# A further pair of weight columns by seven products, and pairs whose second result goes through SBUF, in a one-core hybrid decoder trunk

## The chip, the cores and the metric

The kernel runs on one core of one Trainium2 chip. The metric is the time of one execution on the device, in microseconds (us); the median of several executions is given. A core has five engines that work side by side, each through its own queue in order: TensorE (PE in the profile, with the loading of its weights as PEld), VectorE (DVE), ScalarE (ACT), GpSimd (POOL) and SyncE (SP), which here issues most DMA transfers. SBUF is the on-chip memory, PSUM the memory into which TensorE writes.

## The reference

One layer of a decoder trunk over 256 tokens of width 2048, in float32. A combined input projection feeds two token mixers (a gated delta rule over 16 heads of 128, and a causal pooling mixer); their results are merged through gates, projected out and added; then follows a gated MLP of width 5632 with a causal depthwise convolution.

```python
h = rmsnorm(x, norm_mix_w[l])
proj = jnp.einsum('bsd,de->bse', h, w_in[l])
q, k, v, z, b_raw, a_raw, p_in, g_a, g_b = jnp.split(proj, splits, axis=-1)
qkv = jax.nn.silu(causal_dwconv(jnp.concatenate([q, k, v], axis=-1), conv_qkv_w[l]))
...
o = gated_delta_rule(q, k, v, g_log, beta)
o = rmsnorm(o, gdn_norm_w[l]) * jax.nn.silu(z)          # per head
pooled = causal_multiscale_pool(p_in)                   # 4 groups of 512 channels
y_b = jnp.einsum('bsgc,gcd->bsgd', pooled, pool_w[l]) * pool_scale[l]
mixed = jax.nn.sigmoid(g_a) * y_a + jax.nn.sigmoid(g_b) * y_b
x = x + jnp.einsum('bsd,de->bse', mixed, w_out[l])
h = rmsnorm(x, norm_ffn_w[l])
...                                                     # gated MLP, final norm
```

## The kernel before

**Stages.** The input projection is worked off in four groups of 512 channels (four heads, one pooling window). Each group passes K, Q, V, P (the pooling mixer's input), GB (its gate), Z, the pooling product, and GA (the delta rule's gate), each a product of 256 tokens by 2048 by 512. Then come the output projection, the MLP's up and down projections and the last norm. The delta rule of a group is side work: a generator (`gdn`, line 948 and after) that advances by one step whenever a product calls `side()`; `LATE[g]` is the number of steps that it lets pass before it starts the triangular solve.

**A weight tile.** Weights come in tiles of 128 x 1024 (two blocks of 128 rows by 512 columns). Each is loaded by SP into `raw` (four buffers), rounded by ACT to a high half (`whi`, line 357, a cast) and split by DVE into a low half (`wlo`, line 368, raw minus high). `weights()` does this a few tiles ahead of the product that uses them, in the order of the list `srcs`. A plain tile costs PE twelve matmuls of 128x512 (two blocks, two token halves, and high by high, low by high, high by low: lines 416 to 418 in `gemm_a`).

**A pair by seven products.** Where two columns of weights are multiplied by the same tokens, a stretch of 512 rows of both (four tiles of 128 x 1024: 11, 12, 21, 22, here called the quad) is done by seven products of six matmuls in place of four plain tiles of twelve, a Strassen-like scheme: the operands T1 to T4 are sums of quarters, formed in place by DVE (`up_sum`, line 284), and the tokens' sums are made once. The seven are called T1, 11, T2, 21, T3, 22 and T4; each has its own cast and split. `pair_product` (line 423 and after) issues one of them on line 455 and moves partial results: after T1 ACT copies bank a's half to SBUF (`own`), after 11 ACT copies the other half over, after T2 DVE adds `own` to the half and keeps the sum in SBUF (`u`, line 443), after T3 DVE adds `own` again and writes it into the second bank of PSUM (line 445). At 21 ACT copies u into the second bank. T3 writes the PSUM half that u is read from, so T3 waits for the addition of u.

Such pairs exist before for K and Q of groups 1 to 3, with T1, 11 and T2 set among the last tiles of the GA before (`KQ_FIRST`), 21, T3 and 22 one behind the other (`KQ_MIDDLE`), and the rest among the plain tiles that follow (`KQ_THEN`), and likewise for two columns of the output projection; others stand in the MLP, which the change leaves alone.

**The running sums.** In group 0 the gate's running sums (16 x 256) are written to DRAM (`crd`, line 817), read back spread over the partitions (`crow`, line 969), masked by POOL (line 974), and become decays by eight exponentials on ACT (`dec`, line 982). A convolution's taps on DVE are `cy` (line 934).

**What sets the order.** Most instructions are put in order on each engine by the scheduler of the language from the order of the code and its own costs; `issue_after` adds an edge, and `manual_schedule` keeps the written order.

## Time and profile before

| what | before |
|---|---|
| median of 3 runs | 1524.24 us (1523.72 to 1524.89) |
| profiled execution | 1524.25 us |
| its span, first to last instruction | 1522.5 us |
| granted TensorE clock | 0.999 |
| busy: PE, PEld, DVE, ACT, POOL | 1513.1, 1250.8, 1287.0, 896.1, 75.0 us |
| starts of tiles in group 0: V's last, P's first | 81.68, 84.42 us |

The profiled execution is the median one, within 0.01 us; 1.75 us of it lie around the span. Matmuls overlap, so their durations add up to more than their pace, and the pace is read from their starts. A row of a timeline gives the start, the duration, engine, line and operation, output and inputs; several alike in a row are put together (x2), and behind them in brackets stands the idle time of the engine before the row and what ended it.

### The profile page before, as it was taken

What the parts mean: (1) busy time and instruction counts of PE and PEld (TensorE: products, weight loads), DVE (VectorE), ACT (ScalarE), POOL (GpSimd) and SP (SyncE); (2) the same over time, 40 slices, a digit from 0 to 9 for tenths busy, and PEclk for the clock granted to TensorE, in tenths of its full rate; (3) what the DMA queues carried; (4) which work ended last, traced back from release to release, by engine and by line L of the source; (5) the groups of instructions that cost most, each with busy time, mean ns of one, the idle gap of its engine ahead of it and who ended that gap; (6) DMA issues with size and microseconds to landing.
All of it is one profiled execution on the core that took longest, in us unless ns stands there. A gap on an engine that the chain in (4) does not pass through costs nothing.

```text
span 1522.5 us, 20282 instructions
## 1 busy us (share of the span) xinstructions
PE 1513.1 (99%) x7260; PEld 1250.8 (82%) x7260; DVE 1287.0 (85%) x1799; ACT 896.1 (59%) x1160; POOL 75.0 (5%) x97
## 2 busy tenths in 40 slices
PE   9999999999999999999999999999999999999998
PEld 8888888888878888888888888888888888888886
DVE  6779868888688878888777999999998886989896
ACT  7456556455646456456465676667666665555562
POOL 1000001000100001000000000000000011010100
PEclk9999999999999999999999999999999999999999
DMA  8777647784677747774678656666457468566662
GB/s 277 209 226 221 207 139 225 235 255 115 198 221 218 227 127 219 214 238 154 217 227 303 198 164 218 221 212 216 152 164 238 142 212 276 172 223 219 220 220 100
DMA packets 170099, 313.62 MB, mean 206 GB/s; under 512 B 23650, under 2 KB 27010, under 8 KB 169870
## 3 DMA queue, kind: packets, MB, share of 16 engines
q1 hardware_dynamic: 160864, 283.17, 59.0%
q0 software_dynamic: 7344, 27.27, 5.5%
q10 hardware_dynamic: 1790, 1.89, 0.4%
q8 instruction: 57, 0.93, 0.2%
q14 instruction: 44, 0.36, 0.1%
HBM read 303.33 MB, written 8.95 MB: 205 GB/s over the span
## 4 chain that ended last, share of the span: by engine, by line
PE 98%; DVE 1%; issue 1%; ACT 0%; POOL 0%; POOLq 0%; DVEq 0%
PE psg L455 28%; PE psm L418 14%; PE psm L416 14%; PE psm L417 14%; PE psm L1644 8%; PE psg L1644 7%; PE psm L455 4%; PE psm L606 1%; PE psm L1712 1%; PE psg L505 1%; PE psg L993 1%; DVE wlo L368 1%; PE psg L995 0%; PE psm L521 0%; PE psg L1139 0%
## 5 line engine op out<-in xcount | busy, mean ns | idle before, releaser
L357 ACT CAST whi<-raw 128x1024 fp32r<-128x1024 f32 x400 | 419.9, 1052 | 311.0 <-PE psm L417 157.9
L368 DVE TENSOR_TENSOR wlo<-raw,whi 128x1024 fp32r<-128x1024 f32 x398 | 484.1, 1220 | 119.3 <-ACT whi L357 113.9
L357 ACT CAST whi<-quad 128x1024 fp32r<-128x1024 f32 x217 | 227.9, 1053 | 167.5 <-PE psg L455 46.2
L368 DVE TENSOR_TENSOR wlo<-quad,whi 128x1024 fp32r<-128x1024 f32 x217 | 263.4, 1220 | 39.9 <-ACT whi L357 34.8
L416 PE MATMUL psm<-whi,xhl 128*128 128x512 f32 x384 | 150.0, 391 | 0.0
L417 PE MATMUL psm<-whi,xhl 128*128 128x512 f32 x384 | 149.9, 390 | 0.0
L418 PE MATMUL psm<-wlo,xhl 128*128 128x512 f32 x384 | 139.0, 393 | 0.0
L455 PE MATMUL psg<-whi,fhl 128*128 128x512 f32 x504 | 127.1, 389 | 0.0
L284 DVE TENSOR_TENSOR quad<-quad,quad 128x1024 f32<-128x1024 f32 x92 | 111.9, 1217 | 0.1
L455 PEld LDWEIGHTS psg<-whi,fhl 128*128 128x128 f32 x504 | 94.6, 188 | 19.7
L416 PEld LDWEIGHTS psm<-whi,xhl 128*128 128x128 f32 x384 | 72.1, 188 | 15.0
L417 PEld LDWEIGHTS psm<-whi,xhl 128*128 128x128 f32 x384 | 72.1, 188 | 14.9
L418 PEld LDWEIGHTS psm<-wlo,xhl 128*128 128x128 f32 x384 | 71.7, 188 | 14.6
L455 PE MATMUL psg<-wlo,fhl 128*128 128x512 f32 x252 | 69.8, 389 | 0.0
L455 PE MATMUL psg<-whi,ups 128*128 128x512 f32 x216 | 58.1, 391 | 0.0
L455 PEld LDWEIGHTS psg<-wlo,fhl 128*128 128x128 f32 x252 | 47.3, 188 | 9.9
L1644 PE MATMUL psm<-whi,hhi 128*128 128x512 f32 (+1 forms) x140 | 54.2, 387 | 0.0
L1644 PE MATMUL psm<-whi,hlo 128*128 128x512 f32 (+1 forms) x140 | 53.7, 386 | 0.0
L1644 PE MATMUL psm<-wlo,hhi 128*128 128x512 f32 (+1 forms) x140 | 50.2, 386 | 0.0
L455 PEld LDWEIGHTS psg<-whi,ups 128*128 128x128 f32 x216 | 40.3, 188 | 8.5 <-issue 0.2
L1644 PE MATMUL psg<-whi,hhi 128*128 128x512 f32 (+1 forms) x120 | 46.4, 387 | 0.0
L1644 PE MATMUL psg<-whi,hlo 128*128 128x512 f32 (+1 forms) x120 | 46.1, 386 | 0.0
(495 smaller groups left out, 3001.2 us busy)
## 6 DMA issues: line engine op xcount, KB each, us to landing
raw<-in_w_in_dram SPq DMA_DIRECT2D x212, 512.0 KB, 4.5
raw<-in_w_up_dram SPq DMA_DIRECT2D x104, 512.0 KB, 4.7
quad<-in_w_up_dram SPq DMA_DIRECT2D x72, 512.0 KB, 5.3
raw<-in_w_down_dram SPq DMA_DIRECT2D x56, 512.0 KB, 5.1
quad<-in_w_down_dram POOLq DMA_DIRECT2D x32, 512.0 KB, 5.4
raw<-in_w_out_dram SPq DMA_DIRECT2D x24, 512.0 KB, 3.7
mv<-vrow SPq DMA_DIRECT2D x12, 512.0 KB, 4.9
quad<-in_w_in_dram SPq DMA_DIRECT2D x12, 512.0 KB, 6.8
```

Of the source, the lines that this page charges most:

```text
L284: nc.vector.tensor_tensor(out_, plus_, minus_, op=ALU.subtract)
L357: last_cast[0] = nc.scalar.copy(hi, raw).ins
L368: last_split[0] = nc.vector.tensor_tensor(lo, raw, hi.bitcast(F32), op=ALU.subtract).ins
L416: mm(ps[:, t, :], lh(k, t), hi[:, kk, :], start=(k == 0), stop=False, **seeded)
L417: mm(ps[:, t, :], ll(k, t), hi[:, kk, :], start=False, stop=False, **seeded)
L418: mm(ps[:, t, :], lh(k, t), lo[:, kk, :], start=False, stop=(k == nk - 1), **seeded)
L455: last_product[0] = mm(ps, lhs(kk), w[n][:, kk], stop=False, skip_group_check=True, start=(first and n == 0 and kk == 0 and lhs is high)).ins
L505: nc.tensor.transpose(pt[:, ff, t * P : (t + 1) * P], src[:, t, f * P : (f + 1) * P], ident)
L606: mm(ps_k0[:, t, :], part(k, t), w[:, kk, :], start=(k == 0 and w is hi and part is xh), stop=(k == KD - 1 and w is lo))
L993: mm(pg0, kq[:, h, 0, 0:P], kq[:, h, :, :], start=True, stop=True)
L1644: mm(ps[:, cs], lhs(kk), part_[:, kk, cs], start=(first and kk == 0 and n == 0), stop=(last and kk == 1 and n == 2), skip_group_check=shared)
L1712: nc.tensor.transpose(out_[f // 2][:, f % 2, t * P : (t + 1) * P], e[:, t, f * P : (f + 1) * P], ident)
```

## The change

P and GB of group 0 become a further pair, named "pg": their tiles 0 and 1 (the first 512 rows) of both columns are done by seven products. T1, 11, T2 and T3 stand among V's last tiles, 21, 22 and T4 among P's. Its quads lie in buffers of the later mixed tiles, u and u2 in `w1` and `w2`. In all five pairs of the two projections the result after T3 goes to SBUF (u2) and ACT copies it into the second bank at the product 22; that bank is taken only there. T3 moves ahead of the gate GA, and 21 and 22 stand singly between plain tiles instead of in a row. `LATE[0]` goes from 26 to 19.

```diff
 NR = P // B0
 AHEAD = 2
 WAIT = 5
-LATE = (26, 24, 22, 18)
+LATE = (19, 24, 22, 18)
 NEVER = -1e30
 
 
...
                 for c in range(nk // 2)]
 
     UP_PARTS = ("T1", "11", "T2", "21", "T3", "22", "T4")
-    KQ_FIRST = ("T1", 5, "11", 6, "T2", 7)
-    KQ_MIDDLE = ("21", "T3", "22")
-    KQ_THEN = (2, "T4", 3, 4, 5, 6, 7)
+    KQ_FIRST = ("T1", 5, "11", 6, "T2", 7, "T3")
+    KQ_MIDDLE = ()
+    KQ_THEN = ("21", 2, "22", 3, "T4", 4, 5, 6, 7)
+    PG_FIRST = ("T1", 5, "11", 6, "T2", 7, "T3")
+    PG_THEN = ("21", 2, "22", 3, "T4", 4, 5, 6, 7)
     up_w = {("kq", g): [cols(w_in[0], base + 512 * g, KD) for base in (C_K, C_Q)] for g in range(1, 4)}
+    up_w["pg", 0] = [cols(w_in[0], base, KD) for base in (C_P, C_GB)]
     srcs = []
     for g in range(4):
         for base in (C_K, C_Q, C_V, C_P, C_GB):
...
             if g and base == C_K:
                 srcs += [("up", ("kq", g), step, 0) if isinstance(step, str) else tiles[step]
                          for step in KQ_MIDDLE + KQ_THEN]
+            elif g == 0 and base in (C_V, C_P):
+                srcs += tiles[:5] if base == C_V else []
+                srcs += [("up", ("pg", 0), step, 0) if isinstance(step, str) else tiles[step]
+                         for step in (PG_FIRST if base == C_V else PG_THEN)]
             else:
-                srcs += tiles[2:] if g and base == C_Q else tiles
+                srcs += tiles[2:] if g and base == C_Q or g == 0 and base == C_GB else tiles
             if g == 0 and base == C_K:
                 srcs += [w_in[0, c * 1024 : (c + 1) * 1024, C_B : C_B + P].rearrange("(k p) f -> p k f", p=P)
                          for c in range(2)]
...
     outw = [cols(w_out[0], 512 * c, KD) for c in range(4)]
     OUT = ("out", 1)
     OUT_STEPS = ((0, 6), "T1", (0, 7), "11", (1, 6), "T2", (1, 7), "21", "T3", "22", (2, 2), "T4")
-    OUT_THEN = (2, "T4", 3, 4, 5)
+    OUT_THEN = ("21", 2, "22", 3, "T4", 4, 5)
     up_w["out", 0] = outw[:2]
     srcs += [("up", ("out", 0), step, 0) if isinstance(step, str) else outw[0][step] for step in KQ_MIDDLE + OUT_THEN]
     srcs += outw[1][2:6]
...
     sums_behind[first_part(OUT) - 1] = [(OUT, "T1", 0)]
     for i in range(2):
         quads_behind[first_part(OUT) - 5 + i] = [(OUT, i)]
-    for pair in (("kq", 1), ("kq", 2), ("kq", 3), ("out", 0)):
+    for pair in (("pg", 0), ("kq", 1), ("kq", 2), ("kq", 3), ("out", 0)):
         sums_behind[first_part(pair) - 1] = [(pair, "T1", 0)]
         for i in range(4):
             quads_behind[first_part(pair) - 6 + i] = [(pair, i)]
...
         ch, i = n // 4, (1, 0, 3, 2)[n % 4]
         if c == OUT:
             home = (big if i < 2 else fp).tile([P, 2, 512], F32, tag=OUT_HOMES[i], name=nm("quad"))
+        elif c == ("pg", 0):
+            home = mtile((1, 2, 5, 6)[i], [P, 2, 512], F32, nm("quad"))
         elif isinstance(c, tuple):
             home = mp.tile([P, 2, 512], F32, tag=KQ_HOMES[i], name=nm("quad"))
         else:
...
         else:
             n = {"T1": 0, "T2": 1, "T3": 2, "22": 3}[what]
             high, low = (lambda kk, s=s: s[:, n, kk * P : (kk + 1) * P] for s in sums)
-        if what == "21":
+        if what == ("22" if "home" in bank else "21"):
+            if b is None:
+                b = bank["ps"][1] = pm()
+                nc.scalar.copy(b[:, 1], bank["u2"])
             nc.scalar.copy(b[:, 0], bank["u"])
         w = weights()
         ps = {"T1": a[:, 0], "21": a[:, 0], "22": b and b[:, 0]}.get(what, a[:, 1])
...
         elif what == "11":
             nc.scalar.copy(a[:, 0], a[:, 1])
         elif what == "T2":
-            bank["u"] = mp.tile([P, 512], F32, tag="dec0", name=nm("u"))
+            bank["u"] = mp.tile([P, 512], F32, tag=bank.get("home", ("dec0",))[0], name=nm("u"))
             nc.vector.tensor_tensor(bank["u"], a[:, 1], bank["own"], op=ALU.add)
+        elif what == "T3" and "home" in bank:
+            bank["u2"] = mp.tile([P, 512], F32, tag=bank["home"][1], name=nm("u2"))
+            nc.vector.tensor_tensor(bank["u2"], a[:, 1], bank["own"], op=ALU.add)
         elif what == "T3":
             nc.vector.tensor_tensor(b[:, 1], a[:, 1], bank["own"], op=ALU.add)
 
...
     pair_bank = {}
     mixing = []
 
-    def kq_steps(steps, ps, flush=3):
+    def kq_steps(steps, ps, flush=3, with_side=False):
 
         for step in steps:
             if isinstance(step, str):
                 pair_product(pair_bank, step, (xh, xl), xsums)
+                if with_side:
+                    side()
             else:
                 gemm_a(xh, xl, KD, (step,), ps, flush)
 
...
                     fixed_parts()
 
             later.append(after_k)
-        e = evict(gemm_a(xh, xl, KD), rsh)
+        if g:
+            ps = gemm_a(xh, xl, KD)
+        else:
+            ps = gemm_a(xh, xl, KD, range(5))
+            pair_bank.update(ps=[pm(), None], home=("w1", "w2"))
+            kq_steps(PG_FIRST, ps, 1, True)
+        e = evict(ps, rsh)
         nc.sync.dma_start(vrow[g, SH : SH + S, :].rearrange("(t p) d -> p t d", p=P), e)
         later.append(lambda e=e, g=g, vt2=vt2: v_moved(e, g, vt2))
 
 
         win = WINDOWS[g]
         psb = scales(g)
-        ps = gemm_a(xh, xl, KD)
+        if g:
+            ps = gemm_a(xh, xl, KD)
+        else:
+            ps = pair_bank["ps"][0]
+            kq_steps(PG_THEN, ps, 2, True)
+            other_ps = pair_bank["ps"][1]
+            pair_bank.clear()
         e = evict(ps) if g == 3 else evict(ps, rsh)
         phi = mtile(g, [P, 4, S], F32R, nm("phi"))
         plo = []
...
                 nc.scalar.activation(th[:, t, :], ps[:, t, :], AF.Tanh, scale=rsh[:, t : t + 1])
             return th
 
-        tb = gate(gemm_a(xh, xl, KD), "th")
+        tb = gate(gemm_a(xh, xl, KD) if g else gemm_a(xh, xl, KD, range(2, 8), other_ps, 2), "th")
         yb = mp.tile([P, 2, 512], F32, tag="yb", name=nm("yb"))
         nc.vector.scalar_tensor_tensor(yb, tb, 1.0, psb.unsqueeze(1).to_broadcast([P, 2, 512]),
                                        op0=ALU.add, op1=ALU.mult)
...
             fixed_order = ExitStack()
             fixed_order.enter_context(tc.manual_schedule(engines={mybir.EngineType.PE}))
             ps = gemm_a(xh, xl, KD, range(5))
-            pair_bank["ps"] = pm(), None
+            pair_bank.update(ps=[pm(), None], home=("dec0", "psb"))
             for early_steps in (KQ_FIRST[:1], KQ_FIRST[1:]):
                 for step in early_steps:
                     if isinstance(step, str):
...
                 ending.append(True)
         else:
             ps = gemm_a(xh, xl, KD, range(5))
-            pair_bank["ps"] = pm(), None
+            pair_bank.update(ps=[pm(), None], home=("dec0", "psb"))
             kq_steps(KQ_FIRST, ps, 1)
         ta = gate(ps, "th")
-        if g < 3:
-            pair_bank["ps"] = pair_bank["ps"][0], pm()
-            kq_steps(KQ_MIDDLE, None)
-        else:
-            pair_bank["ps"] = pair_bank["ps"][0], pm()
-            for step in KQ_MIDDLE:
-                first_out(step)
         with tc.issue_after(last_split[0]):
             nc.vector.scalar_tensor_tensor(sz, ta, 1.0, sz, op0=ALU.add, op1=ALU.mult)
         sz4 = sz.rearrange("p t (h d) -> p (t h) d", h=4)
...
     side_work[0] = end(side_work[0])
     osum = big.tile([P, 2, 4, S], F32R, tag="x3", name="osum")
 
-    early = list(pair_bank["ps"])
     for step in OUT_THEN:
         if isinstance(step, str):
             first_out(step)
         else:
-            gemm_a(at(mhi), at(mlo), KD, (step,), early[0], 9)
+            gemm_a(at(mhi), at(mlo), KD, (step,), pair_bank["ps"][0], 9)
+    early = list(pair_bank["ps"])
     for n in range(2):
         nc.scalar.copy(osum[:, n], osums[n])
     gemm_a(at(mhi), at(mlo), KD, range(2, 6), early[1], 9)
```

The engines' queues show what the scheduler makes of it. First DVE in group 0, where V's last tile (wlo_945 before, wlo_1022 now) and P's first (wlo_977 before) are split. Names: cy is a convolution's tap, quad a quarter or a sum of quarters, u the sum after T2, u_184 the sum after T3, psm the product banks. Before:

```order
L934 SCALAR_TENSOR_TENSOR cy_812<-psg_802,cqw,cy_812 128x255
L934 SCALAR_TENSOR_TENSOR cy_812<-psg_802,cqw,cy_812 128x254
L934 SCALAR_TENSOR_TENSOR cy_812<-psg_802,cqw,cy_812 128x253
L368 TENSOR_TENSOR wlo_977<-raw_973,whi_975 128x1024
L934 SCALAR_TENSOR_TENSOR cy_812<-psg_802,cqw,cy_812 128x255
L934 SCALAR_TENSOR_TENSOR cy_812<-psg_807,cqw,cy_812 128x255
L368 TENSOR_TENSOR wlo_1006<-raw_1002,whi_1004 128x1024
```

And now, from the split of T2 to the addition that makes u:

```order
L377 TENSOR_TENSOR wlo_1005<-quad_690,whi_1003 128x1024
L293 TENSOR_TENSOR quad_710<-quad_690,quad_710 128x1024
L949 SCALAR_TENSOR_TENSOR cy_820<-psg_810,cqw,cy_820 128x255
L377 TENSOR_TENSOR wlo_1022<-raw_1018,whi_1020 128x1024
L949 SCALAR_TENSOR_TENSOR cy_820<-psg_815,cqw,cy_820 128x255
L949 SCALAR_TENSOR_TENSOR cy_820<-psg_810,cqw,cy_820 128x254
L377 TENSOR_TENSOR wlo_1053<-quad_710,whi_1051 128x1024
L293 TENSOR_TENSOR quad_690<-quad_762,quad_690 128x1024
L949 SCALAR_TENSOR_TENSOR cy_820<-psg_815,cqw,cy_820 128x254
L949 SCALAR_TENSOR_TENSOR cy_820<-psg_810,cqw,cy_820 128x253
L455 TENSOR_TENSOR u_1062<-psm_950,own_961 128x512
L377 TENSOR_TENSOR wlo_1067<-quad_762,whi_1065 128x1024
```

Two quarter sums (L293) and the splits of T2 and T3 (wlo_1005, wlo_1053) stand there beside the split of V's last tile; u is behind all of them.

Second, ACT at the same place, with the last exponential on the running sums and what follows it. Before:

```order
L982 ACTIVATE dec_133_828<-crow_829,ncum 128x128
L357 CAST whi_975<-raw_973 128x1024
L931 ACTIVATE cy_812<-psg_802,cqw 128x256
L931 ACTIVATE cy_812<-psg_807,cqw 128x256
L357 CAST whi_1004<-raw_1002 128x1024
```

And now:

```order
L997 ACTIVATE dec_137_836<-crow_837,ncum 128x128
L366 CAST whi_1003<-quad_690 128x1024
L946 ACTIVATE cy_820<-psg_810,cqw 128x256
L366 CAST whi_1020<-raw_1018 128x1024
L946 ACTIVATE cy_820<-psg_815,cqw 128x256
```

The first cast behind the exponentials was that of P's first tile and is now that of T2 (whi_1003), with V's last tile (whi_1020) behind it.

Third, PE at the end of GA in group 0, where the pair of group 1 begins: from T2 (whi_1950) to T3 (whi_1980), with the last plain tile of GA (whi_1964) between.

```order
L470 MATMUL psm_1919<-wlo_1952,xs_784 128x512 x2
L427 MATMUL psm_1820<-wlo_1966,xhl_116 128x512
L427 MATMUL psm_1821<-wlo_1966,xhl_116 128x512
L425 MATMUL psm_1820<-whi_1964,xhl_116 128x512
L426 MATMUL psm_1820<-whi_1964,xhl_116 128x512
L427 MATMUL psm_1820<-wlo_1966,xhl_116 128x512
L425 MATMUL psm_1821<-whi_1964,xhl_116 128x512
L426 MATMUL psm_1821<-whi_1964,xhl_116 128x512
L427 MATMUL psm_1821<-wlo_1966,xhl_116 128x512
L470 MATMUL psm_1918<-whi_1993,xhl_115 128x512 x4
L470 MATMUL psm_1919<-whi_1980,xs_784 128x512
```

Before, the delta rule's small matmuls (16 of 32x32 on line 1121 behind T2) stood in this stretch, and the six matmuls of 21 were followed by T3 at once; now eight matmuls of a plain tile and four of 21 are all that separates T2 from T3.

## The prediction

> **What bounds the kernel now.** The first part of the profile's page gives the busy time of each engine, its fourth part the chain of work that ended last; the next view lists what TensorE (PE) waited for.
>
> ```profile
> span 1522.5 us, 20282 instructions
> PE 1513.1 (99%) x7260; PEld 1250.8 (82%) x7260; DVE 1287.0 (85%) x1799; ACT 896.1 (59%) x1160; POOL 75.0 (5%) x97
> PE 98%; DVE 1%; issue 1%; ACT 0%; POOL 0%; POOLq 0%; DVEq 0%
> ...
> engine line waited for: us in total, times, longest us
> PE psm L521 <- POOL ones L511: 1.1, 1, 1.1
> PE psg L455 <- DVE wlo L368: 0.3, 1, 0.3
> PE psm L418 <- DVE wlo L368: 0.2, 1, 0.2
> ```
>
> The chain is 98% PE, and PE waits 1.6 us in the whole run, 1.1 of them once at the start. So there is about 0.5 us that better order could win back, and everything else that shortens the program must take matmuls away. A busy PE is not yet a PE at its pace, so I looked at where its matmuls start, in PE's timeline around the first tiles of P, group 0:
>
> ```profile
> 81.68 0.40 PE L416 MATMUL psm<-whi,xhl 128*128 128x512 f32 x1
> 81.91 0.39 PE L417 MATMUL psm<-whi,xhl 128*128 128x512 f32 x1
> ...
> 84.42 0.39 PE L416 MATMUL psm<-whi,xhl 128*128 128x512 f32 x1
> 84.64 0.39 PE L417 MATMUL psm<-whi,xhl 128*128 128x512 f32 x1
> 84.87 0.39 PE L416 MATMUL psm<-whi,xhl 128*128 128x512 f32 x1
> 85.10 0.40 PE L417 MATMUL psm<-whi,xhl 128*128 128x512 f32 x1
> 85.33 0.62 PE L418 MATMUL psm<-wlo,xhl 128*128 128x512 f32 x2
> ```
>
> Each takes 0.39 us but they overlap: twelve of them start between 81.68 and 84.42, one every 2.74 / 12, about 0.227 us. That is the price of a 128x512 matmul here. The last row also shows how close VectorE (DVE) is behind: the L418 matmul at 85.33 reads the low half of its tile. The timelines of ACT, DVE, POOL and SyncE (SP) at this place say why:
>
> ```profile
> 67.83 3.09 SPq L253 DMA_DIRECT2D raw<-in_w_in_dram  x2
> 70.97 0.46 SPq L817 DMA_DIRECT2D crd<-crs  x1
> 75.38 0.35 SPq L969 DMA_DIRECT2D crow<-crd  x1
> ...
> 79.79 1.22 POOL L974 TENSOR_SCALAR_AFFINE_SELECT crow<-crow 128x512 f32<-128x512 f32 x2 [22.53 <-DMA crow<-crd]
> ...
> 80.46 2.45 ACT L982 ACTIVATE dec<-crow,ncum 128x128 f32<-128x128 f32 x8 [2.92 <-POOL crow L974]
> 82.82 1.04 ACT L357 CAST whi<-raw 128x1024 fp32r<-128x1024 f32 x1
> 83.76 0.82 ACT L931 ACTIVATE cy<-psg,cqw 128x256 f32<-128x256 f32 x2
> ...
> 83.89 1.23 DVE L368 TENSOR_TENSOR wlo<-raw,whi 128x1024 fp32r<-128x1024 f32 x1 [4.80 <-ACT whi L357]
> ...
> 86.95 1.64 DVE L934 SCALAR_TENSOR_TENSOR cy<-psg,cqw,cy 128x254 f32<-128x254 f32 x4
> ...
> 95.63 2.35 DVE L368 TENSOR_TENSOR wlo<-raw,whi 128x1024 fp32r<-128x1024 f32 x2
> ```
>
> The running sums go out to DRAM at 70.97 and are read back at 75.38; POOL masks them at 79.79; ACT stands in front of its eight decay exponentials for 2.92 us, and the cast queued behind them comes at 82.82. DVE, with nothing cast, idles 4.80 us, splits that tile from 83.89 to 85.12, and PE reads it at 85.33. **The lead is 0.2 us here.** The table of stretches then shows whether DVE has room:
>
> ```profile
> 78.00:84.00 6.00, 6.00 (x30) 4.93 (x29) 1.13 (x4) 3.54 (x10) 1.22 (x2) 1.00 0.61 194
> 84.00:96.00 12.00, 12.00 (x55) 9.91 (x54) 11.91 (x17) 8.60 (x12) 0.00 (x0) 1.00 0.64 189
> 96.00:108.00 12.00, 12.00 (x51) 9.29 (x50) 8.56 (x15) 3.04 (x4) 0.00 (x0) 1.00 0.94 314
> 108.00:134.00 26.00, 26.00 (x117) 20.90 (x116) 25.36 (x46) 15.19 (x21) 2.94 (x2) 1.00 0.66 189
> 185.00:200.00 15.00, 15.00 (x117) 11.93 (x116) 14.21 (x21) 8.99 (x13) 0.00 (x0) 1.00 0.24 70
> ```
>
> The columns are busy time of PE, weight loads, DVE, ACT, POOL, then the granted clock (1.00), the DMA share and GB/s. From 84 to 96, where the new pair goes, DVE is busy 11.91 of 12 us; from 84 to 134 it idles 0.09 + 3.44 + 0.64 = 4.2 us.
>
> **The change part by part.** *Matmuls.* Four plain tiles of twelve become seven products of six: 48 to 42. Saved: 6 x 0.227 = **1.36 us**, the only certain term.
>
> *Work added for it.* Prices from the groups of the page and of the lines concerned:
>
> ```profile
> L357 ACT CAST whi<-quad 128x1024 fp32r<-128x1024 f32 x217 | 227.9, 1053 | 167.5 <-PE psg L455 46.2
> L368 DVE TENSOR_TENSOR wlo<-quad,whi 128x1024 fp32r<-128x1024 f32 x217 | 263.4, 1220 | 39.9 <-ACT whi L357 34.8
> L284 DVE TENSOR_TENSOR quad<-quad,quad 128x1024 f32<-128x1024 f32 x92 | 111.9, 1217 | 0.1
> ...
> L443 DVE TENSOR_TENSOR u<-psm,own x4: 690/690/693, 186.7 to 714.6; 128x512 f32<-128x512 f32 x4
> L445 DVE TENSOR_TENSOR psm<-psm,own x4: 698/698/700, 194.8 to 721.6; 128x512 f32<-128x512 f32 x4
> L438 ACT COPY own<-psm x4: 577/578/580, 177.0 to 705.1; 128x512 f32<-128x512 f32 x4
> L432 ACT COPY psm<-u x4: 597/598/601, 190.8 to 719.9; 128x512 f32<-128x512 f32 x4
> ```
>
> DVE gets three more splits (3 x 1.22), four quarter sums (4 x 1.22) and two additions (2 x 0.69): 9.9 us. ACT gets three casts (3 x 1.05) and four copies, one like L438 and three priced as L432: 3.15 + 2.37 = 5.5 us. ACT's time itself is covered (3.04 of 12 us busy from 96 to 108); its order is not. DVE's 9.9 us meet 4.2 us of idle time after 84 and the 4.8 us before it, of which DVE can use only what was cast before ACT stops.
>
> *The walk through the pair.* By the order of the change, ACT's first cast behind the exponentials is now T2's, the next V's last tile; DVE then has in line, ahead of the addition that makes u: three splits and two sums (5 x 1.13, the pitch of 95.63's two, 2.35 - 1.22), five taps (5 x 0.39, the pitch in 86.95's four, (1.64 - 0.47) / 3, one tap being 0.47) and u's own 0.69. If the exponentials come when they did, u is ready at 83.89 + 5.65 + 1.95 + 0.69 = 92.2. PE comes to V's last tile at 81.68 + 2.72 (T1 and 11 stand ahead now) = 84.4, but its cast, behind T2's and one tap, ends near 82.82 + 0.94 + 0.41 + 1.04 = 85.2: 0.8 us of waiting. From there 22 matmuls (four, T2's six, eight, four of 21) take 5.0 us to 90.2, and T3, which writes the bank that u reads, waits until 92.2: 2.0 us. Behind u the split of 21, a tap and the split of P's tile 2 (1.13 + 0.39 + 1.22) end at 94.9, where PE could have read at 92.2 + 8 x 0.227 + 0.45 = 94.5: 0.4. Then the product on vt and the second addition (1.13 + 0.69) hold the second bank till 96.7, PE being there at 94.9 + 6 x 0.227 = 96.3: 0.4. **Sum 3.6 us**, one end of the bounds.
>
> The other end: the running sums may come back sooner. Before, a 512 KB load was issued just ahead of them (the second of the two from 67.83, which end at 70.92). In the changed order the load ahead waits for a split one weight earlier and goes out about 2.7 us sooner, so the way out, 75.38 - 70.97 = 4.41 us, may shorten by anything from nothing to 2.6 us. At 2.6 the first wait is gone, T3 is reached at 84.4 + 5.0 = 89.4 and u is there at 89.6: 0.2 + 0.4 + 0.4 = 1.0 us. I take the middle, 1.3 us sooner: u at 90.9, T3 waits 1.5, the sum is 1.5 + 0.8 = **2.3 us**. As a cross-check by amounts: of 9.9 us about 3.5 (the split of T1 and the sums for T1 and T2) fall before 84, so 6.4 stand against 4.2 us of idle time while PE comes 1.36 us sooner: 3.6 us short, less what DVE starts sooner.
>
> A wait there passes on: it stops the whole of PE, and no later stage gets it back, since PE is the chain.
>
> *The older pairs.* The second result goes to SBUF by 0.690 instead of 0.698 us: nothing. One more copy of 0.60 us on ACT each, with ACT 8.99 of 15 us busy: nothing while DVE isn't waiting for a cast behind it, 0.6 each if it is. T3 now follows T2 with no delta-rule matmuls between in group 1. Before:
>
> ```profile
> 180.35 1.23 DVE L368 TENSOR_TENSOR wlo<-quad,whi 128x1024 fp32r<-128x1024 f32 x1
> ...
> 186.67 0.69 DVE L443 TENSOR_TENSOR u<-psm,own 128x512 f32<-128x512 f32 x1 [0.20 <-PE psm L455]
> ...
> 186.02 0.61 PE L455 MATMUL psm<-wlo,xs 128*128 128x512 f32 x2
> ...
> 190.49 1.07 PE L455 MATMUL psm<-whi,xs 128*128 128x512 f32 x4
> ```
>
> T2's split was done at 181.6, 4.4 us before PE used it, and u at 187.4, 3.1 us before T3. After, DVE has between T2's split and u a sum, two splits, another sum, two small steps and u (5 x 1.13 less one = 4.5, + 0.4 + 0.7 = 5.6 us), PE 14 matmuls (3.2 us): a deficit of 2.4 us that the lead of 4.4 covers, if it is still there; DVE is busy 14.21 of 15 us. Bounds 0 and 2.4; taken **0.4**, near the lower end since the lead shown is the larger number. Groups 2 and 3 and the output pair keep delta-rule matmuls in between: 0. Singly set products can win the waits listed above, 0 to 0.5: taken 0. The four quarter loads carry the bytes of the four tiles they replace; they stand earlier in SP's queue and cost nothing while DMA is busy 61 to 68% of the time; one load late would cost under 0.5.
>
> **Sum:** -1.36 + 2.3 + 0.4 = +1.3 us on the profiled 1524.25, which is the median of 1524.24: **1525.6 us**.
>
> One rule weighs against the change. The Trainium skill, "Perfetto Trace Analysis", section "Identifying the Most-Contended Engine", tells one to judge TensorE not by its matmul rows but by weight-load time, and the other engines by occupancy. Read so, PE stands at 82% and DVE at 85%, and DVE would be the engine to spare. The trace agrees from 84 to 96 only; elsewhere PE waits for next to nothing. What it would make of the time is the last rival.
>
> **The rivals.** (1) *The saving arrives whole.* The sums return 2.6 us sooner, DVE works through its line before PE gets there. For it: DVE's 4.80 us of idle time, and the DMA engines' spare share. Against: the lead of 0.2 us, and the order in which u stands behind five large operations. Time 1524.25 - 1.36 = 1522.9, down to 1522.4 with 0.5 of the old waits. (2) *Slower: u is late in every pair.* T3 is moved up against u in the kq pairs of groups 1 to 3 also; if the leads of 4.4 us have shrunk below 2.4, each T3 waits. It decides at that lead. For it: 14.21 of 15 us in group 1. Against: other matmuls stay in between in groups 2 and 3. With a lead of 1 us, 3 x 1.4 = 4.2 more: 1525.6 - 0.4 + 4.2 = 1529.4. (3) *DVE is the bound throughout*, so that its 9.9 us come on top: 1534.2. Against: the 0.5 us that PE waits after the start. That the change doesn't do what it says I set aside: the order has the 42 matmuls.
>
> **How the numbers follow.** A measurement of this kernel tells 0.2%, 3.05 us, from no change. Forecast 0.52, its own range -0.4 us (1.0 us of waits against 1.36) to +4.6 (3.6 and 2.4 against it), so 1523.9 to 1528.9, about a fifth of it above +3.05. Rival 1 0.24, all but within the bound: even with the old waits it wins 1.9 us. Rival 2 0.21, slower. Rival 3 0.03. Faster: 0.02. Slower: 0.2 x 0.52 + 0.21 + 0.03 = 0.34. Same: 0.64. The range goes from 1522.4, rival 1 with every old wait gone, to 1529.4, rival 2.
>
> **What would show it.** In the changed trace PE has 6 fewer matmuls of 128x512. If I am right, its list of waits names T3 in group 0 waiting on u's addition for 1 to 2 us near 90 us, the exponentials begin between 77.9 and 80.5, DVE stays above 95% busy from 82 to 96, and beyond group 1 both programs run with a constant offset. No wait of PE near 90 us would make rival 1 right; waits at T3 in three groups rival 2. An offset that arises after 730 us, where the order is unchanged, would prove the prediction wrong in kind.

## The result: 16.9 us slower, most of it far from the new pair

The change runs at 1540.95 us in the median of 4 runs (1539.2 to 1542.9), before at 1524.03 (1523.72 to 1524.89, the runs beside it included): a ratio of 1.0111, with a 95% interval of 1.0099 to 1.0124. The forecast was 1525.6, the range 1522.4 to 1529.4. The prediction was wrong.

First the lines of the changed kernel's page that answer to those shown of before (span, busy time, the chain of waits), and the list of what TensorE waited for:

```profile
span 1537.5 us, 20282 instructions
PE 1518.3 (99%) x7254; PEld 1250.4 (81%) x7254; DVE 1292.2 (84%) x1808; ACT 904.7 (59%) x1171; POOL 72.1 (5%) x97
PE 84%; DVE 4%; DMA 2%; issue 1%; ACT 1%; POOL 0%; SPq 0%; POOLq 0%; DVEq 0%; ACTq 0%
...
PE psg L1118 <- DVE T L1094: 6.5, 2, 5.9
PE psm L470 <- DVE u L455: 1.5, 2, 1.3
PE psm L425 <- DVE u L458: 1.2, 1, 1.2
PE psm L536 <- POOL ones L526: 1.1, 1, 1.1
PE psm L427 <- DVE wlo L377: 0.8, 3, 0.4
PE psg L470 <- DVE wlo L377: 0.3, 1, 0.3
```

The six matmuls are gone (7260 to 7254), but in the chain DVE's share has gone from 1% to 4% and DMA has come in with 2%, and the longest wait of all, 5.9 us, is for something the prediction never looked at: T, the transposes of a triangular solve.

To see where the time went I numbered the 128x512 matmuls of both traces (the gram products, which move freely, left out; 6142 and 6136 records) and compared the start of the same one. At each of these points both runs have the same smaller matmuls behind them too.

| at, in before | end of group 0, 163 us | group 1, 312 us | group 2, 496 us | group 3, 679 us | output pair, 713 us | 761 us |
|---|---|---|---|---|---|---|
| the change is behind by | 0.83 | 3.41 | 4.79 | 7.29 | 14.95 | 15.37 |

From there to the end it stays near that: the profiled execution of the change, the fastest of its four, took 1539.2 us, 14.95 more than that of before, and it is these 14.95 that are taken apart here. So in group 0, where most of the prediction's working went, the new pair costs 0.83 us, and the rest comes later, in code that the pair doesn't touch. Of the 6.5 us that groups 1 to 3 lose, the waits that the profile names make 2.6 (the longest is 1.2 us for u2, the sum after T3, in group 1); the rest was not taken apart.

**Group 0**, by rows of the timelines of SP, ACT, DVE and PE of the change:

```profile
70.62 0.34 SPq L832 DMA_DIRECT2D crd<-crs  x1
74.28 0.35 SPq L984 DMA_DIRECT2D crow<-crd  x1
...
78.91 2.45 ACT L997 ACTIVATE dec<-crow,ncum 128x128 f32<-128x128 f32 x8 [1.17 <-POOL crow L989]
...
89.96 0.69 DVE L455 TENSOR_TENSOR u<-psm,own 128x512 f32<-128x512 f32 x1
...
90.70 1.20 PE L470 MATMUL psm<-whi,xs 128*128 128x512 f32 x4 [1.29 <-DVE u L455]
...
84.00:96.00 12.00, 10.55 (x44) 7.75 (x43) 12.00 (x16) 8.01 (x11) 0.00 (x0) 1.00 0.38 119
```

The way of the running sums out of the core took 74.28 - 70.62 = 3.66 us in place of 4.41, the exponentials began at 78.91, u was there at 90.65, T3 waited 1.29 us, and DVE was busy 12.00 of 12 us. The forecast had 77.9 to 80.5, 90.9, 1.5 and above 95%.

**Group 3 and the output pair.** The groups of the small operations of the solve, of its transposes and of the products on them, first of before (min/median/max in ns, then first and last start in us), from 600 to 760 us:

```profile
L1057 DVE TENSOR_TENSOR tmp<-lb,tb x31: 169/215/236, 651.6 to 686.2; 128x60 f32<-128x60 f32 x3, 128x28 f32<-128x28 f32 x2, 128x54 f32<-128x54 f32 x2, 128x48 f32<-128x48 f32 x2
...
L1079 DVE STREAM_TRANSPOSE T<-TT x4: 432/437/442, 695.4 to 697.3; 32x256 f32<-32x256 f32 x4
...
L1103 PE MATMUL psg<-T,ga x32: 191/191/212, 708.6 to 709.1; 32*32 32x32 f32 x32
```

and of the change the group of the solve, with rows of the timelines of SP, DVE and PE:

```profile
L1072 DVE TENSOR_TENSOR tmp<-lb,tb x31: 169/213/238, 667.6 to 710.6; 128x60 f32<-128x60 f32 x3, 128x28 f32<-128x28 f32 x2, 128x54 f32<-128x54 f32 x2, 128x48 f32<-128x48 f32 x2
...
712.76 2.77 SPq L1079 DMA_DIRECT2D tbd<-tb  x4
717.01 1.82 SPq L1082 DMA_DIRECT2D TT<-tbd  x4
...
720.41 1.84 DVE L1094 STREAM_TRANSPOSE T<-TT 32x256 f32<-32x256 f32 x4 [1.42 <-DMA TT<-tbd]
...
721.83 1.07 PE L1118 MATMUL psg<-T,ga 32*32 32x32 f32 x32 [5.87 <-DVE T L1094]
```

Before, the solve ended near 686 us, went through DRAM, was transposed by 697.7, and its products came at 708.6: some 10.8 us in hand. In the change its last step starts at 710.6, 24.4 us later, where PE is only 7.3 us later. PE's order in the output pair is written by hand, so the products keep their place, and everything behind them waits. Once PE had waited, its clock was down; the table of stretches, with the granted clock in the column behind POOL:

```profile
716.00:722.00 6.00, 0.17 (x6) 0.17 (x8) 4.49 (x7) 1.08 (x2) 0.00 (x0) 0.75 0.71 195
722.00:724.00 2.00, 2.00 (x36) 1.84 (x35) 0.72 (x4) 1.03 (x4) 0.00 (x0) 0.50 0.06 23
724.00:726.00 2.00, 2.00 (x7) 1.57 (x6) 0.17 (x2) 0.00 (x0) 0.00 (x0) 0.55 0.04 8
726.00:728.00 2.00, 2.00 (x11) 1.62 (x10) 0.00 (x0) 0.75 (x1) 0.00 (x0) 1.00 0.00 0
```

At 0.50 to 0.55 for four microseconds the next 128x512 matmuls start 0.43 us apart in place of 0.227. Wait and slow clock make 14.95 - 7.29 = 7.7 us there.

### The profile page after: what moved, and what is told of

Read it like the earlier page. It is cut to its first block, busy times and chain, and to the rows that moved or that the text cites. A ratio compares the mean times of both kernels' runs of the same rounds, so it can differ in the third digit from the quotient of the medians.

```text
span 1537.5 us, 20282 instructions
## 1 busy us (share of the span) xinstructions
PE 1518.3 (99%) x7254; PEld 1250.4 (81%) x7254; DVE 1292.2 (84%) x1808; ACT 904.7 (59%) x1171; POOL 72.1 (5%) x97
## 3 DMA queue, kind: packets, MB, share of 16 engines
q10 hardware_dynamic: 1790, 1.89, 0.4%
## 4 chain that ended last, share of the span: by engine, by line
PE 84%; DVE 4%; DMA 2%; issue 1%; ACT 1%; POOL 0%; SPq 0%; POOLq 0%; DVEq 0%; ACTq 0%
PE psg L470 28%; PE psm L427 11%; PE psm L425 11%; PE psm L426 11%; PE psm L1666 7%; PE psg L1666 7%; PE psm L470 4%; DVE wlo L377 2%; PE psm L1734 1%; PE psg L1008 1%; PE psg L520 1%; DMA raw<-in_w_in_dram 1%; DMA TT<-tbd 0%; DVE cy L949 0%; DMA tbd<-tb 0%
## 5 line engine op out<-in xcount | busy, mean ns | idle before, releaser
L366 ACT CAST whi<-quad 128x1024 fp32r<-128x1024 f32 x224 | 235.3, 1053 | 178.2 <-PE psg L470 46.0
L377 DVE TENSOR_TENSOR wlo<-quad,whi 128x1024 fp32r<-128x1024 f32 x224 | 272.2, 1221 | 49.0 <-ACT whi L366 43.1
L426 PE MATMUL psm<-whi,xhl 128*128 128x512 f32 x368 | 145.3, 395 | 0.0
L425 PE MATMUL psm<-whi,xhl 128*128 128x512 f32 x368 | 144.2, 392 | 0.0
L427 PE MATMUL psm<-wlo,xhl 128*128 128x512 f32 x368 | 135.8, 393 | 0.4 <-DVE wlo L377 0.4
L293 DVE TENSOR_TENSOR quad<-quad,quad 128x1024 f32<-128x1024 f32 x96 | 117.0, 1219 | 0.1
L426 PEld LDWEIGHTS psm<-whi,xhl 128*128 128x128 f32 x368 | 69.4, 188 | 14.9 <-issue 0.7
L425 PEld LDWEIGHTS psm<-whi,xhl 128*128 128x128 f32 x368 | 69.5, 189 | 14.5
```

The source lines that it names most:

```text
L293: nc.vector.tensor_tensor(out_, plus_, minus_, op=ALU.subtract)
L366: last_cast[0] = nc.scalar.copy(hi, raw).ins
L377: last_split[0] = nc.vector.tensor_tensor(lo, raw, hi.bitcast(F32), op=ALU.subtract).ins
L425: mm(ps[:, t, :], lh(k, t), hi[:, kk, :], start=(k == 0), stop=False, **seeded)
L426: mm(ps[:, t, :], ll(k, t), hi[:, kk, :], start=False, stop=False, **seeded)
L427: mm(ps[:, t, :], lh(k, t), lo[:, kk, :], start=False, stop=(k == nk - 1), **seeded)
```

## The experiments

### Which part of the change: pair_alone and singles_alone

pair_alone keeps the new pair and gives the four older pairs their old order; singles_alone is the reverse.

```diff
 pair_alone, against the change:
-    KQ_FIRST = ("T1", 5, "11", 6, "T2", 7, "T3")
-    KQ_MIDDLE = ()
-    KQ_THEN = ("21", 2, "22", 3, "T4", 4, 5, 6, 7)
+    KQ_FIRST = ("T1", 5, "11", 6, "T2", 7)
+    KQ_MIDDLE = ("21", "T3", "22")
+    KQ_THEN = (2, "T4", 3, 4, 5, 6, 7)
...
-            pair_bank.update(ps=[pm(), None], home=("dec0", "psb"))
+            pair_bank["ps"] = pm(), None
 singles_alone, against the change:
-LATE = (19, 24, 22, 18)
+LATE = (26, 24, 22, 18)
...
-    up_w["pg", 0] = [cols(w_in[0], base, KD) for base in (C_P, C_GB)]
```

> The new pair of P and GB in group 0 as in the change, LATE[0] at 19; the four older pairs in the order of before (T3, 21 and 22 in a row, second result straight into the second bank). The change ran at 1540.95 us, before at 1524.03. By stages its trace is +1.0 us behind at the end of group 0, +3.4 at 300 us, +4.8 at 490, +7.3 at 645 and +15.0 at 728 us, where TensorE waits 5.87 us for the transposes of group 3's triangular solve. Theory: the new pair loads VectorE in group 0, the delta rule's side work falls behind there and hands the delay on from group to group. Then this run keeps most of the loss: 1533 to 1541 us. Rival: the order of the older pairs alone pushes the side work back; then this run shows only the first +1.0 us: 1524.5 to 1526.

> The four older pairs as in the change (T3 before the gate, 21 and 22 singly, second result by way of SBUF), no new pair, LATE[0] at 26. Theory of the new pair as the cause: group 0 is untouched, so the side work isn't late: 1523 to 1526 us, no long wait of TensorE. Rival, the order of the older pairs as the cause: the wait for the transposes in group 3 is there again, 1532 to 1540 us. If both contribute, 1527 to 1532.

Measured: pair_alone 1541.03 us (1.0116, 1.0099 to 1.0133), with a wait of 5.2 us for the transposes; singles_alone 1524.67 (1.0004, 0.9995 to 1.0014). singles_alone's list of waits is that of before:

```profile
PE psm L531 <- POOL ones L521: 1.1, 1, 1.1
PE psg L465 <- DVE wlo L372: 0.3, 1, 0.3
PE psm L422 <- DVE wlo L372: 0.2, 1, 0.2
```

The new pair is enough for all of it. The second half of the change, the order of the older pairs and the way through SBUF, neither costs nor brings anything in the whole time, without the pair or beside it.

### What of the pair: load_alone

Before, with nothing of the pair but its weight on VectorE: eight subtractions of a buffer from itself.

```diff
                 split_of[len(made)] = last_split[0]
+                if 23 <= len(made) < 31:
...
+                    with tc.issue_after(last_split[0]):
+                        nc.vector.tensor_tensor(idle[0], idle[0], idle[0], op=ALU.subtract)
```

> Before, with eight subtractions of 128x1024 on VectorE added in group 0, one behind the split of each of V's last three and P's first five tiles, on a buffer that nothing else uses: 8 x 1.22 = 9.8 us of VectorE, as much as the new pair adds, and no other part of it (no products, sums of quarters, copies or quarter loads). Theory: the load alone makes group 0's side work late, the delay goes from group to group, and TensorE waits for the transposes of group 3's solve: group 0's gram products come 7 to 12 us later than at 97.8 us, and the time is 1536 to 1545 us. Rival: it is the pair's order (waits of T3, banks, loads); then only the local wait at P's tiles shows, 1524 to 1528 us.

Measured: 1543.34 us (1.0122, 1.0107 to 1.0137). The first lines of its waits, and the group of its solve in group 3:

```profile
PE psg L1110 <- DVE T L1086: 6.5, 2, 5.2
PE psm L425 <- DVE wlo L369: 4.9, 9, 1.4
...
L1064 DVE TENSOR_TENSOR tmp<-lb,tb x31: 171/211/236, 668.7 to 712.3; 128x60 f32<-128x60 f32 x3, 128x28 f32<-128x28 f32 x2, 128x54 f32<-128x54 f32 x2, 128x48 f32<-128x48 f32 x2
```

The eight subtractions took VectorE 10.2 us, between 70 and 98 us. In group 0 itself they cost TensorE nothing (it is 0.04 us ahead of before at 163 us). Yet TensorE waits 5.2 us until 722.8 us, as with the pair, and the solve of group 3 runs from 668.7 to 712.3. So the load on VectorE in group 0 is enough. But how does it reach group 3?

### Is the start of group 0's solve the lever: late26 and late36

LATE[0] alone is changed: to 26 in the change, to 36 in before.

> The change with LATE[0] back at 26 steps, nothing else. If the start of group 0's triangular solve is set by the steps, it starts about 7 steps of 1.36 us later and all later groups are handed that delay: 1542 to 1550 us. If it is set by the data (gram products, the way through DRAM), nothing moves: 1539 to 1543 us.

> Before, with LATE[0] at 36 in place of 26: group 0's triangular solve is let in about ten steps, 8 to 13 us, later, with no work added anywhere. Theory of a chain of side work that hands a delay on: the delta rule of groups 1 and 2 is late by about as much, and in group 3 TensorE waits for the transposes: 1530 to 1542 us. Rival: a delay in one group is taken up by the slack of the next (the solve of group 1 starts at 305.2 us as before): 1523 to 1526 us.

Measured: late26 1542.17 us (1.0118, 1.0103 to 1.0133), the solve of group 0 starting at 141.2 us against 140.8, in both behind an idle time of 1.1 us that the DMA of its operands ended: it starts when its data are there, and the steps don't count. late36 fell between the two ranges: 1529.26 us (1.0035, 1.0021 to 1.0049). Its trace is the odd one. Group 0's solve ends 21 us later than before (192.2 against 171.0), worse than in the change (183.2), and group 1's gram products start 24.7 us later. Yet the solves of groups 2 and 3 start 4.5 and 5.6 us later, where PE itself is 4.5 us late at both, and PE waits nowhere for transposes. A theory in which the chip hands a delay from group to group doesn't fit that, and I gave it up here.

### The delay is in the written queues: late1_16, load_late1_16, late3_24

What the chip does not explain, the queues show before anything runs. I counted, in the order in which VectorE's instructions are written, how many splits of weight tiles stand ahead of the first and the last product (`tmp`) of group 3's solve:

| kernel | first, last product of group 3's solve, in splits | less the pair's own three | longest wait of PE for the transposes of group 3 | median us |
|---|---|---|---|---|
| before | 223, 236 | | none | 1524.0 |
| singles_alone | 223, 236 | | none | 1524.7 |
| late36 | 223, 236 | | none | 1529.3 |
| the change | 228, 245 | 225, 242 | 5.9 | 1541.0 |
| pair_alone | 228, 245 | 225, 242 | 5.2 | 1541.0 |
| load_alone | 225, 242 | | 5.2 | 1543.3 |

With the load in group 0 the scheduler, which orders instructions by its own simulated times, writes group 3's solve two splits later at its start and six at its end. The products on TensorE, fixed by hand, stay. Three runs test this. Each changes one number.

```diff
 late1_16 (against the change)
-LATE = (19, 24, 22, 18)
+LATE = (19, 16, 22, 18)
 load_late1_16 (against load_alone)
-LATE = (26, 24, 22, 18)
+LATE = (26, 16, 22, 18)
 late3_24 (against before)
-LATE = (26, 24, 22, 18)
+LATE = (26, 24, 22, 24)
```

> The change with LATE[1] at 16 in place of 24, nothing else: no work is taken away. In the queues that the scheduler then writes, group 3's solve stands from VectorE's 226th to its 239th split (228 to 245 in the change, 223 to 236 before, three of them being the new pair's own), so three splits behind the order of before at both ends, that is where it was; group 0 is as in the change. Theory A, the delay is carried by the written order of the queues: the wait of 5.87 us and the slow clock behind it go, and groups 2 and 3 lose nothing more; left are about +0.8 us of group 0 and +2.6 of group 1: 1526 to 1529 us. Theory B, the delay is carried on the chip from group to group by the side work being late: group 0 is as late as before, so the time stays at 1538 to 1543 us.

> Before with the eight added operations on VectorE in group 0 (1543.3 us with LATE[1] at 24) and LATE[1] at 16. Its queues put group 3's solve at splits 223 to 236 as before. Theory A (written order): 1526 to 1532 us. Theory B (carried on the chip): 1540 to 1545 us.

> Before with LATE[3] at 24 in place of 18: only group 3's triangular solve is moved, to splits 226 to 244 of VectorE (223 to 236 before), while TensorE's products on the transposes stay at their place in the written order; groups 0 to 2 are as before and no work is added. Theory A: this alone makes TensorE wait in the output pair: before had 708.6 - 697.3 - 0.5 = about 10.8 us between the transposes and their use, eight splits of 2.72 us are 21.8 us, so 11 us of waiting less what VectorE makes good, and some 1.6 us of low clock: 1531 to 1537 us. Theory B (a late group 3 is the end of a chain that began in group 0): 1523 to 1526 us.

Measured: late1_16 1530.07 us (1.0038, 1.0026 to 1.0051), load_late1_16 1527.87 (1.0028, 1.0018 to 1.0038), late3_24 1532.83 (1.0057, 1.0041 to 1.0072). First late1_16, its waits and its solve:

```profile
PE psm L470 <- DVE u L455: 1.7, 2, 1.4
PE psm L425 <- DVE u L458: 1.4, 1, 1.4
...
L1072 DVE TENSOR_TENSOR tmp<-lb,tb x31: 168/216/240, 658.5 to 691.9; 128x60 f32<-128x60 f32 x3, 128x28 f32<-128x28 f32 x2, 128x54 f32<-128x54 f32 x2, 128x48 f32<-128x48 f32 x2
```

Nothing is lighter than in the change, group 0 is as late (its solve ends at 184.5 us), and the wait for the transposes is gone; 10.9 us are back. Group 2, group 3 and what follows lose 0.7, 0.15 and 0.4 us there, in place of 1.4, 2.5 and 8.1 in the change. The time is 1.1 us above the range of theory A, which had put 0.8 us for group 0; it was 2.1. load_late1_16 gets 15.5 us back the same way; its longest wait is for group 0's transposes, at 194 us:

```profile
PE psg L1110 <- DVE T L1086: 1.7, 1, 1.7
...
L1064 DVE TENSOR_TENSOR tmp<-lb,tb x31: 168/215/239, 655.2 to 689.4; 128x60 f32<-128x60 f32 x3, 128x28 f32<-128x28 f32 x2, 128x54 f32<-128x54 f32 x2, 128x48 f32<-128x48 f32 x2
```

Now late3_24, in which no work is added. In the traces the instructions of PE, ACT and POOL stand in the order of before from end to end, and VectorE's order differs only between 651 and 711 us; groups 0 to 2 run as before (0.15 us behind at 706 us). Its busy times, waits, solve and clock:

```profile
PE 1515.7 (99%) x7260; PEld 1252.6 (82%) x7260; DVE 1287.8 (84%) x1799; ACT 896.4 (59%) x1160; POOL 74.7 (5%) x97
...
PE psg L1103 <- DVE T L1079: 6.2, 1, 6.2
...
L1057 DVE TENSOR_TENSOR tmp<-lb,tb x31: 173/214/236, 659.5 to 706.8; 128x60 f32<-128x60 f32 x3, 128x28 f32<-128x28 f32 x2, 128x54 f32<-128x54 f32 x2, 128x48 f32<-128x48 f32 x2
...
709.00:715.00 6.00, 0.00 (x0) 0.00 (x0) 4.21 (x7) 0.94 (x2) 0.00 (x0) 0.71 0.42 92
715.00:717.00 2.00, 1.94 (x35) 1.89 (x36) 0.65 (x3) 1.03 (x4) 0.00 (x0) 0.50 0.77 245
717.00:719.00 2.00, 2.00 (x6) 1.53 (x5) 0.39 (x3) 0.00 (x0) 0.00 (x0) 0.50 0.00 1
```

VectorE is no busier than before (1287.8 against 1287.0), and still 6.2 us of waiting and a clock of 0.50 put the run 9.4 us behind at 744 us. The place of one solve in one queue is enough for the largest part of the loss. My expectation of the wait (11 us) was too large. The solve's last product did come nearly eight tiles later (20.6 us), but the way from there to the end of the transposes took 8.6 us in place of 11.5, so they were done 17.7 us later and not 21.8.

### Can the end be let in later: ending_later

```diff
-            for early_steps in (KQ_FIRST[:1], KQ_FIRST[1:]):
+            for early_steps in (KQ_FIRST[:5], KQ_FIRST[5:]):
```

> The change, but in the output pair the delta rule of group 3 is let into TensorE's written order behind 11, tile 6 and T2 instead of directly behind T1, two plain tiles and two products later (about 8 us). Theory: the wait of 5.87 us goes and with it the low granted clock behind it (0.50 to 0.55 from 722 to 726 us, 1.6 us): 1533 to 1534.5 us. Rival: the delta rule's end is itself what the output projection waits for, so the wait only moves behind it: 1539 to 1542 us.

Measured: 1544.13 us (1.0133, 1.0118 to 1.0148). The rival was right, though the time is 2 us above its range:

```profile
PE psm L470 <- DVE u L455: 4.1, 3, 2.6
PE psg L520 <- DVE sz L1418: 4.0, 1, 4.0
...
PE psg L1118 <- DVE T L1094: 0.5, 1, 0.5
```

The products on group 3's T no longer wait (the 0.5 us left are group 2's, at 546 us). Instead T3 of the output pair waits 2.6 us for u at 726 us, and the output projection waits 4.0 us at 769 us for sz, the output of the delta rule. The end of group 3's delta rule is on the path; here an earlier solve helps and a later use does not.

### Taking load off VectorE: pool_sums and pool_v

```diff
 pool_sums
-                nc.vector.tensor_tensor(out_, plus_, minus_, op=ALU.subtract)
+                (nc.gpsimd if c == ("pg", 0) else nc.vector).tensor_tensor(out_, plus_, minus_, op=ALU.subtract)
 pool_v
-                nc.vector.tensor_tensor(m, m, taps_of[g][j], op=ALU.mult)
-            nc.vector.tensor_tensor(vt, vt, m, op=ALU.add)
+                (nc.vector if g else nc.gpsimd).tensor_tensor(m, m, taps_of[g][j], op=ALU.mult)
+            (nc.vector if g else nc.gpsimd).tensor_tensor(vt, vt, m, op=ALU.add)
```

> The change, with the four quarter sums of the new pair on GpSimd in place of VectorE (4 x 1.22 = 4.9 us off VectorE in group 0). Theory of VectorE's load: u comes about 2.4 us sooner, so T3's wait near 89 us goes, the taps end 4 to 6 us sooner than at 100.4 us, and since before had about 11 us between the transposes of group 3's solve and their use, most of the wait of 5.87 us goes: 1525 to 1533 us. If GpSimd is too slow for it (above 4 us each) T1 or T3 comes late and the time is above 1541 us. Rival (not VectorE's load): no change, 1539 to 1543 us.

> The change, with six operations of V's convolution in group 0 (three products and three additions of 128x1024, 7.3 us) on GpSimd in place of VectorE. They stand beside and behind the taps of K and Q rather than ahead of u. Theory of VectorE's load: the wait at T3 near 89 us stays (1.5 us), the gram products come sooner, and the delay handed on shrinks by up to 7 us: 1525 to 1534 us. Rival: 1539 to 1543 us.

Measured: 1540.53 us (1.0109, 1.0094 to 1.0124) and 1544.53 (1.0135, 1.012 to 1.015). Neither helped. In pool_sums the wait at T3 shrank to 0.7 us and the gram products came 3 us sooner than in the change (104.8 against 108.0), as they should. In pool_v they came 3.2 us later (111.2), against the expectation, and the time is above both of its ranges. The written place of group 3's solve was still 228 to 245, in both, and the wait there 5.4 and 5.5 us. The sums cost GpSimd 2.4 us each, about twice the 1.22 us that they cost VectorE, in its lines from 40 to 140 us:

```profile
L293 POOL TENSOR_TENSOR quad<-quad,quad 128x1024 f32<-128x1024 f32 x4 | 9.6, 2405 | 30.3 <-PE psm L427 16.7 <-DVE wlo L377 13.6
```

The theory of the load gave the wrong numbers here because the load is not what reaches group 3; the order is, and these edits left it as it was.

### What is left: late_16_14_10, t3_later, t3_later_all, pair_alone16

late_16_14_10 is the change with LATE at 19, 16, 14, 10; pair_alone16 is pair_alone with LATE[1] at 16. The other two build on late1_16:

```diff
 t3_later
-    PG_FIRST = ("T1", 5, "11", 6, "T2", 7, "T3")
+    PG_FIRST = ("T1", "11", 5, "T2", 6, 7, "T3")
 t3_later_all, also
-    KQ_FIRST = ("T1", 5, "11", 6, "T2", 7, "T3")
+    KQ_FIRST = ("T1", "11", 5, "T2", 6, 7, "T3")
```

> The change with LATE at 19, 16, 14, 10: the solves of groups 2 and 3 stand a little earlier still (165 to 180 and 226 to 238). If the place of group 3's solve is all that mattered, the time is within 1 us of the run with 19, 16, 22, 18; if an earlier solve crowds the splits of the tiles beside it, 1 to 3 us more.

> The change with LATE[1] at 16, and in the new pair of group 0 the steps before P as T1, 11, 5, T2, 6, 7, T3 in place of T1, 5, 11, 6, T2, 7, T3: two plain tiles (5.4 us) rather than one between T2 and T3, same work. If T3's wait on u (1.4 us near 90 us) is a local lack of time, it goes: 1528 to 1529.2 us. If VectorE is short over the whole of group 0, the wait moves to the next split or to the second addition: 1529.5 to 1531 us.

> The same, and the same steps in the older pairs and the output pair. If the waits of the additions in group 1's pair (1.4 + 0.3 us) are local too, they go as well: 1526.5 to 1528 us. If VectorE is short: 1529.5 to 1532 us.

> The new pair with the older pairs in the order of before, and LATE[1] at 16: the older pairs then have no u2 that stands behind the transposes of group 0 on VectorE, so group 1's wait of 1.4 us goes: 1528 to 1529 us. It had 1541.03 us with LATE[1] at 24. If the new order of the older pairs had helped instead, 1530.5 to 1532 us.

Measured: 1530.63 us (1.0045, 1.0031 to 1.0059), 1531.25 (1.0048, 1.0033 to 1.0063), 1529.93 (1.0031, 1.0017 to 1.0046) and 1529.5 (1.0036, 1.0023 to 1.005). All lie within 2 us of late1_16's 1530.07. late_16_14_10 came out as the place of the solve would have it, t3_later_all as a short VectorE would; t3_later lies 0.25 us above the range for a short VectorE, and pair_alone16 between its two ranges. The waits of t3_later:

```profile
PE psm L425 <- ACT whi L366: 1.8, 1, 1.8
PE psm L536 <- POOL ones L526: 1.1, 1, 1.1
PE psm L427 <- DVE wlo L377: 1.0, 3, 0.4
PE psm L425 <- DVE u L458: 0.7, 1, 0.7
PE psg L1118 <- DVE T L1094: 0.6, 1, 0.6
PE psm L470 <- DVE wlo L377: 0.6, 1, 0.6
```

T3's wait on u is gone from the list and u2's is down to 0.7 us, but now a cast (at 84 us), the transposes of group 0 (at 202 us) and a split behind them wait in their place. In pair_alone16, too, the wait for u2 went as expected, and 1.5 us for the transposes of group 0 came, at 197 us. So the remaining 5.5 to 7 us don't look like one step badly placed. The likeliest reading, which no run settles, is that VectorE's queue is short of time over groups 0 and 1, and a wait that is moved comes out elsewhere. load_late1_16 fits it without any pair: 3.8 us from the added load with the order put back. No version tried beats before.

## Why the prediction was wrong

**Right: the new pair itself.** The forecast for the end of group 0 was -1.36 + 2.3 = +0.9 us; measured +0.83, from a start that was 0.15 us ahead. The middle taken for the running sums (1.3 us sooner) was 0.75 on the way out and about 1.75 at POOL's mask. One plain tile between T2 and T3 being too little was right, and so was what is late next: by PE's starts the split of P's tile 2 and the second addition hold it up by about 0.35 us each, for the 0.4 and 0.4 of the forecast. That the middle was hit so closely is luck. late1_16 and ending_later have the same order on PE, DVE and ACT up to 298 us; there the exponentials began at 80.2 and 80.3, and the end of group 0 lay 2.1 and 2.2 us behind before. That is the forecast's other end, at which the sums come no sooner (-1.36 + 3.6).

**Wrong: "Groups 2 and 3 and the output pair keep delta-rule matmuls in between: 0."** This step, and the 0.4 us for group 1, priced the older pairs by what separates T2 from T3. Measured were 2.6 us in group 1, 1.4 in group 2, 2.5 in group 3 and 8.1 in the output pair, 14.5 in place of 0.4. Little of the price was at T3: the additions of the older pairs' sums were waited for 1.2 us in group 1 and 0.2 at 546 us. Most of it was in the delta rule's side work, whose place in VectorE's queue the change moved in every group, although the diff touches its code in LATE[0] only: late1_16, which puts the later groups back, recovers 10.5 of the 14.5 us. The step that failed left this path out of the sum. singles_alone shows that the edit which this step argued about costs nothing by itself; late1_16 and late3_24 show what does. The loss of group 1 is not explained by it: late1_16 still has 2.8 us there.

**How it was missed.** I read the changed queues at the two places where the diff acts (group 0 and the first older pair), and for the output pair TensorE's queue alone, where the products on T stand as before. VectorE's queue for groups 1 to 3 would have shown the solve of group 3 ending six splits later, 16 us at 2.72 us a tile (against PE it ended 24.4 - 7.3 = 17.1 us later), with 10.8 us in hand: a wait of about 5.5 us, which the run has with 5.9. Both numbers were there before the run. The sentence that "beyond group 1 both programs run with a constant offset" took for granted what had to be looked up: the offset grew from 3.4 us to 15.4.

**The rivals.** None had the mechanism. Rival 2 looked for waits at T3 in the kq pairs: there is one of 1.2 us for u2 in group 1, and little else. Rival 3, VectorE as the bound throughout, came nearest in time (1534.2) but not in kind: late3_24 loses 8.8 us with VectorE no busier than before. The Trainium skill's rule in "Perfetto Trace Analysis", section "Identifying the Most-Contended Engine", by which TensorE stands at its weight-load time and VectorE would be the engine to spare, did point at the right engine, and the change's page agrees with that reading (PEld 81%, DVE 84%). What decided was not how busy VectorE is but what stands where in its queue.

**Still open** is why the scheduler, with a load in group 0, keeps the side work late through two more groups, and falls back into step with LATE[1] at 16 in the change and in load_alone, or with LATE[0] at 36 in before. Its simulated times were not looked into.

## What to carry to other kernels

Where a scheduler writes the queues, a change in one place can reorder another engine's work hundreds of microseconds later; compare the written order of every engine over the whole program, and above all the producers of what a hand-written order waits for. TensorE at 99% busy says nothing of a second chain beside it: ask how many microseconds each side chain has in hand where it joins (here 10.8), and price an edit against that. When a small edit loses much, try the same load without the edit, and the same shift without the load: the two together tell work from order.

## What the runs showed of the hardware

A long wait of TensorE cost more than its length here. After 5.9 us the granted clock was 0.50 to 0.55 for about 4 us and the loss was 7.7 us in all; after 6.2 us in late3_24 it was down for another 6.7 us, and the loss was 9.3. In the traces' records of the granted clock the stretches at 0.50 last 6.83 us in the change and 10.24 us in late3_24, waits included, and 3.41 us in t3_later: two, three and one times the same length. The Trainium skill, "TensorE: Matmul & The Clock Gate", section "What's actually happening", has the clock go to half after an idle window of about 3.4 us; these two runs agree. But t3_later shows a drop where no wait was that long, in its table of stretches:

```profile
200.00:202.00 2.00, 1.50 (x7) 0.92 (x5) 1.31 (x4) 1.16 (x2) 0.00 (x0) 1.00 0.70 243
202.00:204.00 2.00, 1.29 (x35) 1.17 (x36) 1.97 (x3) 0.23 (x1) 0.00 (x0) 1.00 0.00 0
204.00:206.00 2.00, 2.00 (x8) 1.53 (x8) 2.00 (x3) 1.84 (x5) 0.00 (x0) 0.71 0.06 10
206.00:208.00 2.00, 2.00 (x6) 1.62 (x5) 1.74 (x5) 0.00 (x0) 0.00 (x0) 0.50 0.91 257
```

Two waits of 0.6 us and 34 small matmuls in four microseconds, with TensorE busy 2.79 of 4.00 us, came before that 0.50. One wait of 1.78 us, at 84 us in the same run, was also followed by 0.50, from 85.4 to 88.8 us. In the change, a wait of 1.29 us among full-size matmuls (84 to 96 us) left the clock at 1.00, and so did one of 1.89 us in pair_alone16. What decides was not found.
